# First attention head loaded by GpSimd, plain FFN units stored raw, two more w_o tiles kept, a new order at the tail

## The chip, the cores and the metric

The kernel runs on one core of a Trainium2 chip. The metric is the time of one execution on the device in microseconds (us), as the median of several. The engines run side by side, each through its own instructions in order, and wait for each other by semaphores: TensorE (matmuls), VectorE, ScalarE, GpSimd, and SyncE (SP), which here only issues DMAs. The profile is one execution seen by the hardware profiler. In it PE is TensorE, PEld its weight loads, DVE VectorE, ACT ScalarE, POOL GpSimd, SPq the queue of SP.

## The reference

One layer of a streaming encoder on 1024 prompt frames and 32 frames of running streams (1056 columns in all), model width 1024, in fp32:

```
p = x @ w_in                  # conv GLU pair | q | k | v | forget logits | 2 x gate
conv:  a*sigmoid(b) -> causal depthwise conv, 31 taps -> LayerNorm -> swish -> w_conv_out
attn:  softmax(q.k/8 + sum of log forget gates, causal) @ v -> w_attn_out   # 8 heads of 64
m   = sigmoid(g_conv)*y_conv + sigmoid(g_attn)*y_attn
x1  = LN1(alpha*x + m @ w_o)
x2  = LN2(alpha*x1 + relu(x1 @ w_up)^2 @ w_down)       # 4096 hidden channels
```

The rows k, v, log f and the last conv inputs are outputs too.

## The kernel before

Activations lie transposed: a tile holds 128 channels on partitions and frames along the row. Each fp32 operand is split into a high and a low half ("hi" by a ScalarE copy into fp32r, "lo" by a VectorE subtraction), and each product is three matmuls (hi hi, hi lo, lo hi), written by `mm3` and `dense`. A generator-driven planner (`Issue`, with a clock of its own for each engine) fixes the order of the instructions on TensorE, VectorE, ScalarE and GpSimd as the program text runs: background work is slipped in when its planned due time has come (`service`, `due`), filler work for TensorE when an operand isn't due yet (`fill`). A `margin` adds to a due time. The DMAs on SP get their order from the framework's scheduler, and run strictly in it.

**Stages.** (1) To 245 us: the input projections; VectorE runs the 31-tap convolution over `u` and `ca` in the background, on into stage 2. (2) To 325: gate tiles 0 to 5. Each gate product is copied from PSUM to `gt` by ScalarE and stored to DRAM (`g_s`). (3) 325 to 590: attention, head by head, with the rest of the gate products as filler; here `gt` has two buffers, and two PSUM banks ("acc") take the filler's products. Head h needs `k1, q1, k2, q2, v`, loaded by `load_head`; rows 64 to 127 of k2 and q2 hold constants (k2 ones; q2 zeros with two rows of ones) and the cumulated forget gates. The SBUF pool "b" of this stage begins where the pools "conv" and "a" lay; a tile waits for what was there. While GpSimd is the split engine (`W.engine = "pool"`) it computes the low halves of weights. (4) To 667: merge. (5) To 762: `w_o`, column blocks of 264 frames in the groups (0, 2), (1,), (3,). Weights pass through a ring of 4 raw and 4 split tiles (`Weights`: `load`, `split`, `take`, `limit` for how far it may read ahead); the odd w_o tiles are kept for all groups, the even ones (0, 2, 4, 6) loaded and split again for each. LN1 of each block runs in the background (`norm_steps`; `emit` makes `x_bh`, `x_bl`). (6) To 838: the plain FFN units: hidden tiles f = 0 to 5 for 4 blocks, 24 products `up`, each Relu, Square, hi, lo, stored to `hp_s` (`rest`, `second_half`, tile "spp"). The first 16 Relu results are held in tiles "d0", "d1". `combine` prepares sums for the next stage. (7) 838 to 1350: the rest of the FFN by a seven-product scheme (`S.step` makes the split weights, `go`/`product` the products in 4 PSUM bank pairs, VectorE adds them up; `residual` adds alpha*x1 as `extra`, one step per product). (8) To the end: `combined` sums, the plain units' down-projection `ps_dn` for three column blocks of 352 (`down_first`, `more`), with the w_down tiles `wd` (two for each pair of output tiles), and LN2 with the last block written out separately.

A gate product is stored by `g = staging.tile([P, CH], F32, tag=tag, bufs=bufs, ...)`, `act(g, ps, AF.Copy)`, `dma(g_s[m, :, chunks[c]], g)`. LN2's due times have `margin = 0.0 if tag >= MUS else NMARGIN` with NMARGIN = 2000 (ns).

Of the kernel before, what the change touches and what calls it, by code (L numbers as in the profile page):

```python
# [17 lines left out]
P = 128  # L18
# [54 lines left out]
NPL = 3  # L73
PAIRS = (*range(4, 15), 3, 15)
# [11 lines left out]
class Issue:  # L86
# [186 lines left out]
def hybrid_layer(ctx: ExitStack, tc, io):  # L273
# [24 lines left out]
    hp_s = [tc.dram_tile([P, 2, T], F32, name=f"hp{i}_s") for i in range(4 * (NFB - NKB))]  # L298
# [21 lines left out]
    plan += [io["w_o"][m] for _ in range(2) for m in range(0, KD, 2)]  # L320
# [487 lines left out]
    with pool("b") as pb, pool("pb", space=PSUM) as psb:  # L808
        k2s, q2s = [], []
        for i in range(2):  # L810
# [7 lines left out]
        sq = [pb.tile([P, 2 * (P + DEC)], F32R, name=f"sq{i}") for i in range(2)]  # L818
        sqv = [t.rearrange("p (n x) -> p n x", n=2)[:, :, 0:DEC] for t in sq]
        sq1, sq2 = ([t[:, 0:P], t[:, P:2 * P]] for t in sq)  # L820
        for t in sq:
            nc.gpsimd.memset(f32(t), 0.0)
        dma(sqv[1][DH:DH + 2], k2s[0][DH:DH + 2, 0:2 * DEC].rearrange("p (n x) -> p n x", n=2))
# [7 lines left out]
        def load_s():  # L831
            for i, t in enumerate(("sh", "sl")):
                for k in range(4):
                    yr[t].append(row(4 * i + k, f"y{t}{k}"))
            for cs in chunks:
                for k in range(4):
                    for i, t in enumerate(("sh", "sl")):
                        dma(yr[t][k][:, cs], s_s[i][k, :, cs])

        def early():  # L840
            for k in range(min(3, len(folded) // 2)):
                load_o(k)
            for m in range(YM):
                yw.append(W.take())
                yc.append(row(14 + m, f"yc{m}", F32))
                for c in range(NCH):
                    terms = y_terms(0, m, c)
                    yield [t for t4 in terms for t in t4]
                    ps = bbank(f"yc{m}_{c}")[:, :CH]
                    for last in mm3(ps, terms):  # L850
                        if not last:
                            yield None
                    act(yc[m][:, chunks[c]], ps, AF.Copy)
                    yield None

        I.filler.append([gates(range(GA, 16), bbank, pb, "g", GB, load_s), None])
        I.filler.append([early(), None])

        def load_head(h, i):
            hr = slice(h * DH, (h + 1) * DH)
            k1 = pb.tile([P, 2 * NKS], F32R, tag="k1", bufs=2, name=f"k1_{h}")
            q1 = pb.tile([P, SEQ], F32R, tag="q1", bufs=2, name=f"q1_{h}")
            k2, q2 = k2s[i % 2], q2s[h % 2]
            v = pb.tile([P, 10, P], F32R, tag="v", bufs=2, name=f"v_{h}")
            dma(k1[0:DH, 0:SEQ], qk_s["kh"][hr, 0:SEQ])
            dma(k1[DH:P, 0:SEQ], qk_s["kh"][hr, 0:SEQ])
            dma(q1[0:DH], qk_s["qh"][hr, 0:SEQ])
            dma(q1[DH:P], qk_s["ql"][hr, 0:SEQ])  # L870
            dma(k2[0:DH, 0:SEQ], qk_s["kl"][hr, 0:SEQ])
            dma(k2[DH:DH + 2, 0:SEQ].rearrange("s (t i) -> s t i", i=P), crows[0][h, :, 0:NT, :])
            dma(q2[0:DH], qk_s["qh"][hr, 0:SEQ])
            dma(q2[DH + 2:DH + 4, :].rearrange("s (t i) -> s t i", i=P), crows[1][h, :, 0:NT, :])
# [4 lines left out]
        def load_cached(g, i):  # L879
            k1 = pb.tile([P, 2 * NKS], F32R, tag="k1", bufs=2, name=f"sk1_{g}")  # L880
            k2 = k2s[i % 2]
            v = pb.tile([P, 10, P], F32R, tag="v", bufs=2, name=f"sv_{g}")
# [38 lines left out]

        units = []
# [4 lines left out]
        loaded = {}  # L927
# [164 lines left out]
        def work():  # L1092
            load(0)
# [135 lines left out]
    with pool("ps1", space=PSUM) as bank_pool[0]:  # L1229
# [54 lines left out]
        with pool("l1") as ln_pool[0]:  # L1284
            LNW, LNQ = CB, 2
            xrs = []
# [56 lines left out]
            for group in GROUPS:  # L1343
                sums = {}
                for m in range(KD):
# [11 lines left out]
                    if m % 2:  # L1357
# [17 lines left out]
            ws, pending, held_r = [], [], []  # L1375

            def rest():

                if pending:
                    r, f, b = pending.pop(0)  # L1380
                    act(r, r, AF.Square)
                    sp = ln_pool[0].tile([P, 2, CB], F32R, tag="spp", bufs=3, name=f"spp{f}_{b}")
# [14 lines left out]
            for n, (f, b) in enumerate(order):  # L1397
# [22 lines left out]
                for _ in range(0 if n < 8 else 1 if 12 <= n < 16 or n > 18 else 2):  # L1420
# [39 lines left out]
    loaded, hs = {}, []  # L1460
# [426 lines left out]
```

## Time and profile before

| | us |
|---|---|
| median of 3 runs | 1474.54 (1473.98 to 1475.47) |
| the profiled execution | 1471.28 |
| its span, first to last instruction | 1469.5 |
| TensorE busy | 1434.3 |
| VectorE busy | 1135.2 |
| ScalarE busy | 678.5 |
| GpSimd busy | 153.1 |

Busy times are of one engine over the span and overlap each other. The mean granted TensorE clock was 0.992 of full speed. A wait is listed as the engine and tile that waited, what released it, the total, the count and the longest. A row of a timeline is start, length, engine, line, operation, tiles and shapes, and in brackets the idle time before it.

### The profile page before, as it was taken

How to read it: one execution, taken by the hardware profiler on the slowest of the kernel's cores; microseconds unless marked ns; L12 is line 12 of the kernel's file. 1: busy time of each engine (PE TensorE's matmuls, PEld its weight loads, DVE VectorE, ACT ScalarE, POOL GpSimd, SP SyncE). 2: the span in 40 equal slices, each digit the busy share in tenths (PEclk: the TensorE clock that was granted, in tenths of full speed). 3: DMA queues.
4: the chain of work that ended last, by engine and by line, in shares of the span. 5: the costliest groups of instructions: out<-in, count | busy, mean ns of one | idle time of the engine just before them, and what ended most of it. 6: DMA issues, size and time to landing. Idle time of an engine off the chain costs nothing.

```text
span 1469.5 us, 28027 instructions
## 1 busy us (share of the span) xinstructions
PE 1434.3 (98%) x10632; PEld 1408.5 (96%) x10632; DVE 1135.2 (77%) x1925; ACT 678.5 (46%) x1425; POOL 153.1 (10%) x203
## 2 busy tenths in 40 slices
PE   9999999998999999999999999999999999999996
PEld 8999999997989999999999999999999999999995
DVE  6999899864666655856697988888976788879668
ACT  5113433455655656533356766676657322213223
POOL 0000000003355543000000000000000000000125
PEclk9999999999999999999999999999999999999998
DMA  7125544267555557435353448766689887775112
GB/s 244 45 67 155 171 167 151 89 219 197 157 146 139 153 148 263 140 99 177 109 166 119 144 153 296 253 240 234 226 295 343 328 323 253 274 270 175 44 40 79
DMA packets 156277, 267.87 MB, mean 182 GB/s; under 512 B 22506, under 2 KB 79082, under 8 KB 156142
## 3 DMA queue, kind: packets, MB, share of 16 engines
q1 hardware_dynamic: 156142, 266.08, 54.7%
q8 instruction: 84, 1.38, 0.4%
q14 instruction: 51, 0.42, 0.1%
HBM read 169.30 MB, written 96.66 MB: 181 GB/s over the span
## 4 chain that ended last, share of the span: by engine, by line
PE 86%; DVE 7%; ACT 2%; DMA 2%; issue 2%; SPq 0%; POOL 0%; DVEq 0%; ACTq 0%; POOLq 0%
PE ps_u L211 18%; PE ps_d L211 15%; PE ps_g L211 10%; PE ps_o L211 6%; PE ps_dn L211 4%; PE ps_v L211 4%; PE ps_yc L211 3%; PE ps_k L211 3%; PE ps_glua L211 3%; PE ps_q L211 3%; PE ps_glub L211 3%; PE ps_s L211 3%; PE ps_yo L211 2%; PE ps_pv L211 2%; PE ps_up L211 2%; PE ps_tr L215 2%
## 5 line engine op out<-in xcount | busy, mean ns | idle before, releaser
L240 DVE SCALAR_TENSOR_TENSOR ca<-u,prm,ca 128x1086 f32<-128x1086 f32 x120 | 161.7, 1347 | 2.4
L223 ACT ACTIVATE swhi<-s 128x512 fp32r<-128x512 f32 x100 | 61.7, 624 | 170.4 <-DVE s L232 154.0
L211 PE MATMUL ps_g<-xh,whi 128*128 128x352 f32 x384 | 132.4, 345 | 7.2 <-ACT gt L223 7.2
L211 PE MATMUL ps_g<-xh,wlo 128*128 128x352 f32 x384 | 124.2, 324 | 0.0
L211 PE MATMUL ps_g<-xl,whi 128*128 128x352 f32 x384 | 122.0, 324 | 0.0
L211 PE MATMUL ps_u<-tl,swhi 128*128 128x264 f32 x416 | 118.4, 285 | 0.0
L211 PE MATMUL ps_u<-th,swlo 128*128 128x264 f32 x416 | 118.3, 284 | 0.0
L211 PE MATMUL ps_u<-th,swhi 128*128 128x264 f32 x416 | 118.2, 284 | 0.0
L223 ACT ACTIVATE whi<-raw 128x512 fp32r<-128x512 f32 (+1 forms) x132 | 76.3, 623 | 65.5 <-PE ps_glua L211 31.6
L232 DVE TENSOR_TENSOR tl<-ps_tr,th 128x512 fp32r<-128x512 f32 (+2 forms) x96 | 51.0, 552 | 58.4 <-ACT th L223 57.7
L223 ACT ACTIVATE r<-r 128x528 f32<-128x528 f32 (+1 forms) x128 | 77.1, 602 | 37.8 <-DVE r L232 35.5
L211 PE MATMUL ps_d<-hu_h,swhi 128*128 128x264 f32 x480 | 92.9, 285 | 0.4 <-DVE aux L232 0.4
L211 PE MATMUL ps_d<-hu_l,swhi 128*128 128x264 f32 x480 | 92.8, 285 | 0.0
L232 DVE TENSOR_TENSOR wlo<-raw,whi 128x512 fp32r<-128x512 f32 (+1 forms) x112 | 72.6, 686 | 22.1 <-ACT whi L223 20.9
L232 DVE TENSOR_TENSOR r<-r,ps_u 128x528 f32<-128x528 f32 x91 | 62.6, 700 | 29.7 <-PE ps_u L211 29.4
L232 POOL TENSOR_TENSOR lnsum_n<-acc,acc 128x352 f32<-128x352 f32 x2 | 1.9, 943 | 790.8 <-DVE acc L232 790.8
L211 PEld LDWEIGHTS ps_g<-xh,whi 128*128 128x128 f32 x384 | 73.2, 191 | 8.3 <-ACT gt L223 7.5
L211 PEld LDWEIGHTS ps_u<-th,swhi 128*128 128x128 f32 x416 | 78.3, 188 | 0.0
L211 PEld LDWEIGHTS ps_u<-th,swlo 128*128 128x128 f32 x416 | 78.3, 188 | 0.0
L211 PEld LDWEIGHTS ps_u<-tl,swhi 128*128 128x128 f32 x416 | 78.2, 188 | 0.0
L211 PEld LDWEIGHTS ps_d<-hu_h,swhi 128*128 128x128 f32 x480 | 74.6, 189 | 0.6 <-issue 0.6
L211 PEld LDWEIGHTS ps_d<-hu_l,swhi 128*128 128x128 f32 x480 | 74.6, 189 | 0.0
(420 smaller groups left out, 5032.3 us busy)
## 6 DMA issues: line engine op xcount, KB each, us to landing
h_s<-sp SPq DMA_DIRECT2D x84, 528.0 KB
raw<-in_w_in_dram SPq DMA_DIRECT2D x64, 256.0 KB
hu_h<-h_s SPq DMA_DIRECT2D x30, 528.0 KB
hu_l<-h_s SPq DMA_DIRECT2D x30, 528.0 KB
sraw<-in_w_up_dram SPq DMA_DIRECT2D x52, 256.0 KB
hu<-h_s SPq DMA_DIRECT2D x24, 528.0 KB
sraw<-in_w_ds_dram SPq DMA_DIRECT2D x48, 256.0 KB
g_s<-gt SPq DMA_DIRECT2D x48, 176.0 KB
```

The lines of the kernel that those rows point to most:

```text
L211: self.nc.tensor.matmul(ps, lhsT=w, rhs=x, start=start, stop=stop)
L215: self.nc.tensor.transpose(ps, x, ident)
L223: self.nc.scalar.activation(out, in_, func, **kw)
L232: (self.nc.vector if eng == "dve" else self.nc.gpsimd).tensor_tensor(out, a, b, op)
L240: self.nc.vector.scalar_tensor_tensor(out, a, s, b, op0, op1)
```

## The change

- Head 0's loads move from SP's queue to GpSimd's, except v's, and are written ahead of the other attention work; the pool's first tiles are now k2_0, q2_0, k1_0, q1_0, v_0, then k2_1, q2_1 and the `sq` tiles. The ones of k2 and q2 are written by GpSimd memsets; three small DMAs that copied ones go.
- In the plain FFN, units f = 0 to 3 are stored raw after their Relu (`hp_s` one half as large); they are loaded again late (`late_hs`, from block 4, second half, step 3 on), squared and split there. Units 4 and 5 keep the old way.
- w_o tiles 2 and 4 are kept too, in "d0" and "d1"; only 0 and 6 are loaded again.
- LN2's due times get the margin of 2000 ns.
- One PSUM bank pair is passed over at the start of the down products; w_down is read ahead by another schedule, and four tiles instead of two are taken before the last `combined` sums.

```diff
+NLATE = 4
+WO_AGAIN = (0, 6)
-    def dma(self, out, in_):
+    def dma(self, out, in_, queue=None):
...
-        self.nc.sync.dma_start(out, in_)
+        (queue or self.nc.sync).dma_start(out, in_)
...
-    plan += [io["w_o"][m] for _ in range(2) for m in range(0, KD, 2)]
+    plan += [io["w_o"][m] for _ in range(2) for m in WO_AGAIN]
...
+        def constants(i):
             k2 = pb.tile([P, 2 * NKS], F32R, name=f"k2_{i}")
-            nc.vector.memset(f32(k2[DH:P, :]), 1.0)
+            nc.gpsimd.memset(f32(k2[DH:P, :]), 1.0)
             q2 = pb.tile([P, SEQ], F32R, name=f"q2_{i}")
             nc.gpsimd.memset(f32(q2[DH:P, :]), 0.0)
-            dma(q2[DH:DH + 2, :], k2[DH:DH + 2, 0:SEQ])
+            nc.gpsimd.memset(f32(q2[DH:DH + 2, :]), 1.0)
...
+            queue = nc.gpsimd if h == 0 else None
-            dma(k1[0:DH, 0:SEQ], qk_s["kh"][hr, 0:SEQ])
+            dma(k1[0:DH, 0:SEQ], qk_s["kh"][hr, 0:SEQ], queue)
...
             dma(v[:, 0:NT, :], v_s[h])
...
+        constants(0)
+        first_head = load_head(0, 0)
+        constants(1)
...
+        for t in sq:
+            nc.gpsimd.memset(f32(t), 0.0)
+        nc.gpsimd.memset(f32(sqv[1][DH:DH + 2]), 1.0)
...
-        margin = 0.0 if tag >= MUS else NMARGIN
+        margin = NMARGIN
...
+            for n, m in enumerate(m for m in range(0, KD, 2) if m not in WO_AGAIN):
+                kept[NWO + m] = lambda n=n, m=m: [ln_pool[0].tile([P, T], F32R, tag=f"d{n}", bufs=2, name=f"{x}_wo{m}") for x in ("whi", "wlo")]
...
-                if n < 16:
-                    if n % 4 == 0:
-                        held_r.append(ln_pool[0].tile([P, T], F32, tag=f"d{n // 8}", bufs=2, name=f"r{n}"))
-                    r = held_r[-1][:, n % 4 * CB:(n % 4 + 1) * CB]
+                r = tmp("rp", 5, f"r{f}_{b}")
+                act(r, ps, AF.Relu)
+                if f < NLATE:
+                    dma(hp_s[f][:, cblocks[b]], r)
                 else:
-                    r = tmp("rp", 3, f"r{f}_{b}")
-                act(r, ps, AF.Relu)
-                pending.append((r, f, b))
+                    pending.append((r, f, b))
...
+    def late_hs():
+        last = []
+        for f in range(NLATE):
+            hs[f] = unit(f"hs{f}", 6 + f)
+            parts = [[t[:, n * 2 * CB:(n + 1) * 2 * CB] for t in hs[f]] for n in range(2)]
+            raw = [pd.tile([P, 2 * CB], F32, tag="x1r", bufs=2, name=f"hr{f}_{n}") for n in range(2)]
+            if last:
+                tt(*last.pop(), SUB)
+            for n in range(2):
+                dma(raw[n], hp_s[f][:, n * 2 * CB:(n + 1) * 2 * CB])
+            yield
+            for n in range(2):
+                act(raw[n], raw[n], AF.Square)
+                act(parts[n][0], raw[n], AF.Copy)
+            tt(parts[0][1], raw[0], f32(parts[0][0]), SUB)
+            last.append((parts[1][1], raw[1], f32(parts[1][0])))
+            yield
+        tt(*last.pop(), SUB)
...
+        pair_bank("skip")
         for kb in range(NKB):
...
-                    if kb == NKB - 1 and g == 0 and 0 < i < 6:
-                        load_hs(i - 1, 5 + i)
+                    if (kb, g, i) == (NKB - 2, 1, 3):
+                        extra = chain(extra, late_hs())
...
-                        W.limit = NPLAN + (1, 1, 2, 3, 3, 4, 5)[i]
+                        W.limit = NPLAN + (1, 1.5, 1.5, 2, 3, 4, 4)[i]
                         W.ahead()
-        for _ in range(2):
+        for _ in range(4):
             wd.append(W.take())
```

## Rows read from the trace of the kernel before

**Rows 1.** The page: busy us, share of the span, instructions; DMA queues.

```profile
PE 1434.3 (98%) x10632; PEld 1408.5 (96%) x10632; DVE 1135.2 (77%) x1925; ACT 678.5 (46%) x1425; POOL 153.1 (10%) x203
...
q1 hardware_dynamic: 156142, 266.08, 54.7%
```

**Rows 2.** Busy time by stage: us, busy us (instructions), clock, DMA share, GB/s.

```profile
667.00:762.00 95.00, 95.00 (x778) 94.67 (x778) 72.51 (x159) 37.21 (x72) 0.00 (x0) 1.00 0.52 161
...
838.00:1330.00 492.00, 492.00 (x4039) 492.00 (x4040) 404.12 (x640) 243.98 (x426) 0.00 (x0) 1.00 0.75 264
```

**Rows 3.** Waits: TensorE's over the span, ScalarE's 333 to 341; us, times, longest.

```profile
PE ps_g L211 <- ACT gt L223: 7.2, 1, 7.2
...
PE ps_dn L211 <- DVE wk_l L232: 2.2, 1, 2.2
...
PE ps_var_n L211 <- DVE lnvar_n L232: 2.0, 2, 1.0
...
PE ps_dn L211 <- DVE acc L232: 1.3, 2, 0.9
...
ACT gt L223 <- DMA g_s<-gt: 14.0, 1, 14.0
```

**Rows 4.** Busy time by stage, around the first head.

```profile
286.40:300.00 13.60, 13.60 (x87) 13.60 (x86) 10.96 (x14) 7.04 (x13) 0.00 (x0) 1.00 0.34 116
...
300.00:325.60 25.60, 25.60 (x162) 25.45 (x161) 17.69 (x34) 15.30 (x32) 0.37 (x1) 1.00 0.72 235
...
340.60:344.60 4.00, 3.95 (x15) 3.85 (x16) 0.92 (x4) 2.05 (x6) 2.52 (x2) 0.50 0.44 123
```

**Rows 5.** The chain of waits, 285 to 341: start us, us, what.

```profile
285.75 0.61 PE ps_var_c L211 x2
...
317.21 1.86 DMA g_s<-gt
...
326.24 6.65 DMA k<-kh_s
...
334.97 5.06 DMA g_s<-gt
...
340.65 2.13 PE ps_g L211 x6
```

**Rows 6.** GpSimd's timeline, to 330: start us, us, operation, its idle time before.

```profile
264.55 0.95 POOL L814 MEMSET q<- 64x1024 f32 x1 [124.05 <-DVE ca L240]
...
315.95 0.37 POOL L822 MEMSET sq<- 128x320 f32 x1 [50.02 <-DVE csl L232]
```

**Rows 7.** Busy time by stage, around 800 us.

```profile
798.70:802.00 3.30, 1.61 (x7) 0.91 (x6) 2.53 (x8) 2.53 (x7) 0.00 (x0) 1.00 0.73 249
...
802.00:805.40 3.40, 3.39 (x14) 3.22 (x15) 3.22 (x7) 1.29 (x3) 0.00 (x0) 0.50 0.56 196
```

**Rows 8.** The chain of waits, around 798 us.

```profile
797.85 2.67 DMA hp_s<-spp
```

**Rows 9.** Timelines of VectorE and of TensorE, 778 to 798 us.

```profile
778.29 0.90 DVE L240 SCALAR_TENSOR_TENSOR acc<-acc,prm,rstd_n 128x264 f32<-128x264 f32 x2
...
784.89 0.49 DVE L240 SCALAR_TENSOR_TENSOR x_1l<-acc,prm,x_1h 128x264 fp32r<-128x264 f32 x1 [0.18 <-ACT x_1h L223]
...
793.07 0.49 DVE L240 SCALAR_TENSOR_TENSOR acc<-acc,prm,rstd_n 128x264 f32<-128x264 f32 x1
...
797.78 0.28 PE L211 MATMUL ps_up<-x_3h,whi 128*128 128x264 f32 x1
```

**Rows 10.** Busy time, the stretch in which the changed kernel squares late.

```profile
1300.70:1327.00 26.30, 26.30 (x218) 26.30 (x217) 21.18 (x34) 5.37 (x9) 0.00 (x0) 1.00 0.60 217
```

**Rows 11.** VectorE's timeline, 1354 to 1366 us.

```profile
1354.57 0.70 DVE L232 TENSOR_TENSOR acc<-acc,aux 128x528 f32<-128x528 f32 x1
...
1365.22 1.28 DVE L232 TENSOR_TENSOR wk_l<-raw,wk_h 128x512 fp32r<-128x512 f32 x2
```

**Rows 12.** Busy time, the last block's end.

```profile
1442.00:1456.00 14.00, 13.18 (x72) 11.20 (x70) 12.21 (x23) 5.37 (x11) 5.48 (x6) 1.00 0.08 27
```

More of the change, by code (lines that the diff above doesn't have):

```diff
@@ L297, in hybrid_layer @@
     h_s = [[tc.dram_tile([P, 2, 2, 2, CB], F32, name=f"h{b}_{i}_s") for i in range(7)] for b in range(NKB)]
-    hp_s = [tc.dram_tile([P, 2, T], F32, name=f"hp{i}_s") for i in range(4 * (NFB - NKB))]
+    hp_s = [tc.dram_tile([P, T] if i < NLATE else [P, 2, T], F32, name=f"hp{i}_s") for i in range(4 * (NFB - NKB))]
     o_s = [tc.dram_tile([H * DH, T], F32, name=f"o{i}_s") for i in range(2)]
@@ L828, in bbank @@
             return psb.tile([P, 512], F32, tag="acc", bufs=2, name="ps_" + name)
[L831 to L854, printed above, removed]
@@ L874, in load_head @@
-            dma(q2[DH + 2:DH + 4, :].rearrange("s (t i) -> s t i", i=P), crows[1][h, :, 0:NT, :])
+            v = pb.tile([P, 10, P], F32R, tag=f"v{i % 2}", bufs=1, name=f"v_{h}")
+            queue = nc.gpsimd if h == 0 else None
+            dma(k1[0:DH, 0:SEQ], qk_s["kh"][hr, 0:SEQ], queue)
+            dma(k1[DH:P, 0:SEQ], qk_s["kh"][hr, 0:SEQ], queue)
+            dma(q1[0:DH], qk_s["qh"][hr, 0:SEQ], queue)
+            dma(q1[DH:P], qk_s["ql"][hr, 0:SEQ], queue)
+            dma(k2[0:DH, 0:SEQ], qk_s["kl"][hr, 0:SEQ], queue)
@@ L920, in load_cached, with load_s, early @@
             return k1, k2, sq1, sq2, v
+        constants(0)
+        first_head = load_head(0, 0)
+        constants(1)
+        sq = [pb.tile([P, 2 * (P + DEC)], F32R, name=f"sq{i}") for i in range(2)]
+        sqv = [t.rearrange("p (n x) -> p n x", n=2)[:, :, 0:DEC] for t in sq]
+        sq1, sq2 = ([t[:, 0:P], t[:, P:2 * P]] for t in sq)
+        for t in sq:
+            nc.gpsimd.memset(f32(t), 0.0)
+        nc.gpsimd.memset(f32(sqv[1][DH:DH + 2]), 1.0)
+        def load_s():
+            for i, t in enumerate(("sh", "sl")):
+                for k in range(4):
+                    yr[t].append(row(4 * i + k, f"y{t}{k}"))
+            for cs in chunks:
+                for k in range(4):
+                    for i, t in enumerate(("sh", "sl")):
+                        dma(yr[t][k][:, cs], s_s[i][k, :, cs])
+        def early():
+            for k in range(min(3, len(folded) // 2)):
+                load_o(k)
+            for m in range(YM):
+                yw.append(W.take())
+                yc.append(row(14 + m, f"yc{m}", F32))
+                for c in range(NCH):
+                    terms = y_terms(0, m, c)
+                    yield [t for t4 in terms for t in t4]
+                    ps = bbank(f"yc{m}_{c}")[:, :CH]
+                    for last in mm3(ps, terms):
+                        if not last:
+                            yield None
+                    act(yc[m][:, chunks[c]], ps, AF.Copy)
+                    yield None
+        I.filler.append([gates(range(GA, 16), bbank, pb, "g", GB, load_s), None])
+        I.filler.append([early(), None])
         units = []
@@ L926, in hybrid_layer @@
                 units.append(("cached", h - 2))
-        loaded = {}
+        loaded = {0: first_head}
         def load(n):
@@ L1092, in work @@
         def work():
-            load(0)
             for n, (kind, h) in enumerate(units):
@@ L1356, in hybrid_layer @@
                         W.drop()
-                    if m % 2:
+                    if m not in WO_AGAIN:
                         wk[m] = w
@@ L1381, in rest @@
                     act(r, r, AF.Square)
-                    sp = ln_pool[0].tile([P, 2, CB], F32R, tag="spp", bufs=3, name=f"spp{f}_{b}")
+                    sp = ln_pool[0].tile([P, 2, CB], F32R, tag="spp", bufs=2, name=f"spp{f}_{b}")
                     act(sp[:, 0, :], r, AF.Copy)
@@ L1419, in hybrid_layer @@
                         next(sums, None)
-                for _ in range(0 if n < 8 else 1 if 12 <= n < 16 or n > 18 else 2):
+                if len(pending) > 1:
                     rest()
@@ L1458, in x_op @@
         return get
-    loaded, hs = {}, []
+    loaded, hs = {}, {}
     places = [("quad", 2 + n, 0) for n in range(2)] + [("quad", n, half) for half in range(2) for n in range(2)]
@@ L1663, in hybrid_layer @@
                         load_h()
-                    if kb == NKB - 1 and g == 0 and 0 < i < 6:
-                        load_hs(i - 1, 5 + i)
+                    if (kb, g, i) == (NKB - 2, 1, 3):
+                        extra = chain(extra, late_hs())
+                    if (kb, g, i) == (NKB - 1, 0, 6):
+                        for _ in extra:
+                            pass
+                        for f in range(NLATE, 5):
+                            load_hs(f, 6 + f)
                     if end:
```

31 lines of the change are left out of this document (9 added, 22 removed).

## The prediction

> **What bounds the kernel now.** I read the page's table of busy time first: TensorE is busy in 1434.3 of 1469.5 us [rows 1], so at most 35 us can be had, and only where TensorE stands or runs slowly. The table by stage shows where it doesn't: from 667 to 762 us and from 838 to 1330 us it is busy in every microsecond [rows 2]. Work that the change takes from VectorE or ScalarE there gives nothing. The list of what TensorE waited for [rows 3] names the rest: one wait of 7.2 us for a gate tile, 2.2 us for the split of a w_down tile, twice 1.0 us for a variance, and 1.3 us in two waits for PSUM banks of the last matmuls. Two more stretches are in the windows: at half the granted clock (1.2 GHz) it ran from 340.6 to 344.6 us, behind the 7.2 us wait [rows 4], and from 802.0 to 805.4 us, behind a stretch of 3.3 us in which it was busy for 1.61 [rows 7].
>
> **Part A, the first head's loads.** TensorE's 7.2 us wait is for the ScalarE copy of a gate bank, and that copy waited 14.0 us for the store of an older gate tile to land (there are two such tiles) [rows 3]. The store was issued at 334.97 and took 5.06 us; a sister issued at 317.21 took 1.86 [rows 5]. It came so late because SP works in order: the head's loads stand ahead of it from 326.24 [rows 5]. The change takes eleven DMAs out of SP's way there: two copies of ones into q2, one into sq, and eight loads of head 0; only v's load stays. The store is then issued some 8.5 us earlier, at about 326.5. Even if it still takes 5.06 us it has landed at 331.6, before TensorE runs out of banks at 333.4 (it went on at 340.65 [rows 5], less 7.2). So the wait goes whole, 7.2 us, and with it the slow clock: 3.95 us of work at half rate is 2.0 us lost [rows 4]. Sum: 9.2 us.
>
> Are the loads themselves in time? On GpSimd they stand behind the memsets of k2 and q2. The new layout puts k2_0, q2_0, k1_0 and q1_0 over the old mean tile and the conv inputs. The conv inputs are free by 264.6, when the second q2 memset ran in the kernel before [rows 6]; the mean tile is last read by the variance matmul that ends at 286.4 [rows 5]. Three memsets of about 0.95 us each [rows 6] bring GpSimd to 289.3. No DMA of the kernel before was issued by GpSimd (queue q1 is SP's alone [rows 1]), so its price has to be bounded: from below by nothing, from above by 5.06 us each, the slowest landing here, if one waited for the other: 8 x 5.06 + 289.3 = 329.8. The first scores come about 334 (in the kernel before they followed six gate matmuls behind the wait [rows 5]). I take 1.5 us each, near the longest GpSimd memset of that kind; done by about 303. Cover is some 30 us, and the whole price is hidden; the DMA engines are at 0.34 and 0.72 of their time from 286 to 325 [rows 4]. GpSimd then waits for the last conv tiles (about 324; the sq memset at 315.95 waited for such a one [rows 6]), does four more memsets and is free by 329. Behind these stands only its next weight split, 2.5 us, which in the kernel before ran at 341 [rows 4]. What is late next is the softmax chain of head 0, as it was before.
>
> The Trainium skill, SBUF — State Buffer, section "SBUF: two separate sides", speaks against this part: descriptors of a DMA that GpSimd issues can't be written while VectorE runs an operation in a two-port mode, such as a plain fp32 copy. VectorE is busy in 10.96 of 13.6 us and in 17.69 of 25.6 us of the stretch [rows 4], but with two-input operations and reciprocals, for which the same page (its summary by port) names no two-port mode for tensor_tensor. No GpSimd DMA in the trace of before shows it. By that rule at its worst the loads go out only after VectorE's last operation; what this would cost is the slower rival below.
>
> **Part B, the plain FFN units.** From 798.7 to 802.0 TensorE lost 1.7 us, and the slow clock after it another 1.7 (half of 3.39) [rows 7]. It waited for the last normalised block, whose ScalarE steps stood behind "spp" tiles waiting for a store to land, 2.67 us [rows 8]. In the changed kernel 16 of the 24 units make no such tile: ScalarE does their Relu alone, 32 activations and 16 VectorE subtractions are gone, and SP stores the raw tile. Without them VectorE goes through the block as it did through the one before it, 16 operations in 7.1 us (from 778.29 to 785.38) from 793.07 on [rows 9]: done by 800.2. TensorE came to the block at 797.78 [rows 9] and takes three matmuls of 492 / 4039 = 0.122 us [rows 2] per tile, so it needs the eighth at 800.3. Sum: 3.4 us; between 1.7 (a rest of the wait keeps the clock low) and 4. Two more w_o tiles kept spare eight halves of a load and a split, all where TensorE is full [rows 2]: nothing.
>
> The work comes back in the last block of the FFN: eight halves are loaded raw, squared, copied (ScalarE is busy in 5.37 of 26.3 us there) and subtracted: 8 x 0.70 (the row of 128 x 528 [rows 11]) = 5.6 us of VectorE between 1300.7 and 1327, where it is busy in 21.18 of 26.3 us [rows 10]. It fits only just: 5.1 us were free. A product of 12 matmuls takes 1.46 us and there are four bank pairs, so TensorE feels a lag only after three products, 4.4 us; nothing is lost there, but I let VectorE enter the next stretch 1 us late (0 to 3).
>
> **Part C, the start of the last matmuls.** From 1330 to 1366 VectorE is the bound. Its order puts the last two "combined" groups (1354.57 to 1365.2) ahead of the split of w_down tile 3 (the first is tile 0) at 1365.22 [rows 11], and TensorE waits 2.2 us for it [rows 3]. With four tiles taken first, the split comes 10 us earlier, and the skipped bank pair makes the first banks wait for an older addition (the longer of those two waits, 0.9 us [rows 3]). TensorE went on about 1365.9 and had 24 matmuls of 0.16 us (25.6 us / 162 of the same width [rows 4]) to tile 4, 1369.8; it now gets there 3.1 us earlier, at 1366.7. Then tile 4's split is late: it follows the combined groups, which two more halves push to 1366.5, so its first half (0.64) ends at 1367.1, a wait of 0.4. Less 1 us brought from part B: 1.7, or 2 us where one of the smaller waits goes as well (from -1 to 3.5).
>
> **Part D, the margin in the last norms.** Both matmuls of a norm are now placed 2 us later than planned. The two waits of 1.0 us go [rows 3]. The first chain has room. The second one ends up to 4 us later, and VectorE has work for 12.21 of the 14 us to 1456 [rows 12], so the outputs of block 1 that haven't been written by then compete with the last block: from 0 to 4 us of it come back at the end. I take 1.5. Sum: a gain of 0.5 (from -2 to 2).
>
> **The sum.** 9.2 + 3.4 + 2.0 + 0.5 = 15.1 us. The profiled execution took 1471.28 us around its span of 1469.5; less 15.1 it would take 1456.2. The median of the runs shown is 3.26 us above that execution, so the median to expect is 1459.4 us.
>
> **Rivals.**
> 1. VectorE full. The late squares put TensorE on hold in the last FFN block, and the second norm's delay comes back whole. For it: 5.1 us free against 5.6 needed. Against it: four bank pairs and weights split four products ahead. Parts C and D are then -1 and -2: 9.2 + 3.4 - 3 = 9.6 us gained, 1464.9.
> 2. Another wait takes the head's place. The gate stores are no longer held, but something else is not there at 333 (head 0's v, still on SP, or a gate weight): half of part A returns with the slow clock. 4.6 + 5.9 = 10.5 gained, 1464; if the whole returns, 5.9, 1468.6. Against it: nothing else waited at that point [rows 3], and the tiles that v covers are free by about 316 [rows 6].
> 3. Slower: GpSimd's issue starves. Its loads start only when VectorE's conv work ends, about 324.4, and cost d each in a row: TensorE waits 324.4 + 8d + 5.06 - 334.2 = 8d - 4.7 us, and 2 us of slow clock. This is worse than the 9.2 us it replaces and the 5.9 gained elsewhere from d = 2.2 us on. At 3 us it gives 19.3 + 2 - 15.1 = 6.2 us slower, 1480.7. At 1.6 it still leaves 5 us gained, 1469.4. For it: no row prices d. Against it: 2.2 us would be over twice a GpSimd memset of 64 x 1024 [rows 6].
> 4. The change doesn't reach what it names: the slow clock stays in both places (3.7 us) though the waits go. 1463.
>
> Another rule, DMA: Bandwidth & Descriptors, section "Issuing engines are not separate DMA queues", says that issuing from another engine saves only the sequencer's time, since all transfers share the same 16 DMA engines. By it the 5.06 us landing need not shorten. The sum above holds with that landing too.
>
> **How the numbers follow.** The forecast as worked out, 1455 to 1463: 0.63. Rival 1: 0.13; rival 2: 0.10; rival 4: 0.04; rival 3: 0.05, of which 0.04 slower than before. The last 0.05 is for better than 1455, where nothing of parts C and D comes back (9.2 + 4 + 3.5 + 2 = 18.7 gained, 1455.8) and one of the waits I have not named goes too. The range from 1453.5 to 1467 leaves out less than 2 in 10. About 0.2% (3 us) is what a measurement of this kernel can tell from no change. Faster by more than that: 0.93; within: 0.03; slower: 0.04.
>
> **What would show it.** In the changed kernel's trace: no TensorE wait for a gate copy near 333 and full clock from 325 to 360 (A); eight GpSimd DMAs issued from about 289, landed well before 334; no wait for x_3 and full clock around 800 (B); VectorE close to full from 1285 to 1315 with no TensorE wait for it; no wait for w_down tile 3, a short one for tile 4 (C); no waits at the variances, and outputs of block 1 among the last block's additions (D). I am wrong if TensorE still stands at the first scores, if GpSimd takes over 2 us per load, or if TensorE waits on VectorE in the last FFN block.

## The result, and the profile after

The changed kernel takes 1464.17 us (median of 4, 1461.97 to 1467.44), the kernel before beside it 1474.87: ratio 0.993, 95% interval 0.991 to 0.9949. So 10.7 us were gained (7.5 to 13.3) where 15.1 were forecast; the time lies in the range of the prediction, but outside its forecast case (1455 to 1463), and next to the prices of two rivals: 1464.9 of rival 1 (VectorE full) and 1464 of rival 2 (half of part A lost), of which the waits below leave only the first. A later set of runs of the same kernel gave 1463.21 (E11).

First the page's table of busy time and the queue that is new, and then the longest of TensorE's waits (total, times, longest), of the changed kernel; the one of 1.9 us for `tl` and two of 1.0 us and less for `yg` that are left out stand in the kernel before too:

```profile
PE 1433.0 (98%) x10632; PEld 1409.1 (96%) x10632; DVE 1126.6 (77%) x1906; ACT 672.5 (46%) x1403; POOL 160.7 (11%) x215
...
q0 software_dynamic: 544, 1.59, 0.4%
```

```profile
PE ps_md_last L213 <- DVE lnsum L234: 4.1, 1, 4.1
PE ps_dn L213 <- DVE acc L234: 2.0, 1, 2.0
...
PE ps_d L213 <- DVE aux L234: 1.7, 1, 1.7
...
PE ps_d L213 <- ACT hs L225: 1.4, 1, 1.4
```

The 7.2 us for a gate tile, the 2.2 us for the split of w_down tile 3 and both waits for a variance [rows 3] are gone, and so is the wait for x_3 near 800 us, which the kernel before had:

```profile
PE ps_up L211 <- ACT x_3h L223: 1.3, 1, 1.3
```

Four others stand in their place, 4.1 + 2.0 + 1.7 + 1.4 = 9.2 us, all in the last 150 us. Where each stands, from TensorE's timeline (start, us, what, and in brackets the idle time before it):

```profile
1315.47 0.48 PE L213 MATMUL ps_d<-hu_h,swhi 128*128 128x264 f32 x2 [1.44 <-ACT hs L225]
...
1335.24 0.48 PE L213 MATMUL ps_d<-hu_h,swhi 128*128 128x264 f32 x2 [1.71 <-DVE aux L234]
...
1345.69 0.43 PE L213 MATMUL ps_dn<-hs_h,whi 128*128 128x352 f32 x1 [2.02 <-DVE acc L234]
...
1445.58 1.12 PE L213 MATMUL ps_md_last<-lnsum,mean_d 128*128 128x352 f32 x2 [4.13 <-DVE lnsum L234]
```

The next table is worked out from the records of TensorE's matmuls in all thirteen traces: the time from the end of the last matmul of one kind to that of the next. "head" runs from the conv norm's last variance to the last score, "up" is norm 1 with the up products of the plain units, "down" the ps_d products, "last" the ps_dn products, "end" from there to the last variance. The stretches that it leaves out agree within 0.7 us, but for the first 17 us of an execution, which differ by up to 2.7 us between these thirteen.

```
us                          head    up     down   last    end
                        var_c-s   o-up    u-d   d-dn   dn-var_last
before                   283.97  75.52  246.69  102.94  2.62
before, second trace E8  287.92  77.01  248.23  104.50  2.63
changed                  275.36  71.11  250.37   99.84  7.71
changed, second     E11  274.86  71.10  250.15   98.29  7.72
E1                       274.73  71.10  249.92  101.54  2.62
E2                       276.31  71.10  247.48   99.84  7.83
E3                       274.69  71.10  248.44   99.96  7.96
E4                       286.38  71.10  252.02   99.91  7.85
E5                       274.75  71.10  249.63  100.23  2.63
E6                       274.73  71.10  249.58  100.21  7.71
E7                       274.75  71.10  248.15   99.10  2.63
E9                       275.02  74.92  248.09   97.23  7.97
E10                      274.68  71.10  248.04   97.58  3.65
```

The first two columns are part A and part B near 800 us, and they gained 8.6 and 4.4 us between the two first traces, where 9.2 and 3.4 were forecast. Of the last three columns together the kernel before needed 352.25 us in its first trace, the changed one 357.92 and 356.16: what parts B (its late half), C and D did from 1100 us on cost 4 to 6 us, where a gain of 2.5 was forecast. From the last score to the last w_o product both kernels take 191.4 us: the two more w_o tiles that are kept gain nothing there, as forecast.

### The profile page after: what moved, and what is told of

It reads as the page before. It is cut to its first block, busy times and chain, and to the rows that moved or that the text cites. A ratio compares the mean times of both kernels' runs of the same rounds, so it can differ in the third digit from the quotient of the medians.

```text
span 1462.5 us, 27944 instructions
## 1 busy us (share of the span) xinstructions
PE 1433.0 (98%) x10632; PEld 1409.1 (96%) x10632; DVE 1126.6 (77%) x1906; ACT 672.5 (46%) x1403; POOL 160.7 (11%) x215
## 4 chain that ended last, share of the span: by engine, by line
PE 89%; DVE 6%; DMA 2%; ACT 2%; issue 1%; SPq 0%; POOL 0%; DVEq 0%; ACTq 0%
PE ps_u L213 18%; PE ps_d L213 14%; PE ps_g L213 10%; PE ps_o L213 6%; PE ps_dn L213 5%; PE ps_up L213 5%; PE ps_v L213 4%; PE ps_glub L213 3%; PE ps_yc L213 3%; PE ps_k L213 3%; PE ps_glua L213 3%; PE ps_q L213 3%; PE ps_s L213 3%; PE ps_yo L213 2%; PE ps_pv L213 2%; PE ps_tr L217 2%
## 5 line engine op out<-in xcount | busy, mean ns | idle before, releaser
L225 ACT ACTIVATE whi<-raw 128x512 fp32r<-128x512 f32 (+1 forms) x120 | 69.4, 623 | 69.3 <-PE ps_glua L213 31.6
L225 ACT ACTIVATE r<-r 128x528 f32<-128x528 f32 (+1 forms) x112 | 70.6, 630 | 38.4 <-DVE r L234 36.2
L234 DVE TENSOR_TENSOR wlo<-raw,whi 128x512 fp32r<-128x512 f32 (+1 forms) x100 | 64.8, 686 | 25.9 <-ACT whi L225 24.7
```

What stands on the lines that cost most here:

```text
L225: self.nc.scalar.activation(out, in_, func, **kw)
L234: (self.nc.vector if eng == "dve" else self.nc.gpsimd).tensor_tensor(out, a, b, op)
```

## The experiments

E1 to E11 below. Each time stands beside runs of the kernel before on the same chip (medians 1473.83 to 1474.58), as a ratio with its 95% interval; the stage lengths are in the table above.

**E1, no margin in the last norms.**

```
-        margin = NMARGIN
+        margin = 0.0 if tag >= MUS else NMARGIN
```

> The margin of 2 us is taken out of the last norms again (as before), all else as in the changed kernel (1464.2 us). Theory M (the margin moves block 1's outputs behind the last block's additions and so makes the new 4.1 us TensorE wait for lnsum): that wait goes, the two waits of 1.0 us for the variances return: 4.1 - 2.0 = 2 us faster, 1462. Theory L (the 4.1 us are VectorE's lag out of the late squares, carried to the end): the wait stays and the two of 1.0 us return: 2 us slower, 1466.

Measured: 1460.87 us, 0.9918 (0.9904 to 0.9931). The 4.1 us are gone and the two waits of 1.0 us are back, as theory M has it; theory L falls. The longest of TensorE's waits of this kernel:

```profile
PE ps_dn L213 <- DVE acc L234: 2.5, 2, 2.0
PE ps_var_n L213 <- DVE lnvar_n L234: 2.0, 2, 1.0
```

From the last ps_d matmul to the last variance this kernel takes 104.16 us, the changed one 106.01 in E11, whose clock stayed up at the start of the last matmuls as it did here: the margin costs 1.85 us.

How it does that is seen in VectorE's order around the last block's first step. "lnpart" is subtracted there from the last block's tiles, and "rstd_n" is the factor of block 1's outputs. The kernel before, and then the changed one:

```profile
1431.31 2.35 DVE L244 RECIPROCAL rstd_n<-rstd_n 128x352 f32<-128x352 f32 x1 [1.54 <-ACT rstd_n L223]
1433.77 1.31 DVE L240 SCALAR_TENSOR_TENSOR acc<-acc,prm,rstd_n 128x352 f32<-128x352 f32 x1
...
1440.42 0.97 DVE L236 TENSOR_SCALAR acc<-acc,prm 128x352 f32<-128x352 f32 x1
1441.32 2.45 DVE L232 TENSOR_TENSOR acc<-acc,lnpart 128x352 f32<-128x352 f32 x2
```

```profile
1423.98 2.35 DVE L246 RECIPROCAL rstd_n<-rstd_n 128x352 f32<-128x352 f32 x1 [2.25 <-ACT rstd_n L225]
1428.45 1.71 DVE L234 TENSOR_TENSOR acc<-acc,lnpart 128x352 f32<-128x352 f32 x2 [2.12 <-ACT lnpart L225]
...
1437.60 1.27 DVE L242 SCALAR_TENSOR_TENSOR acc<-acc,prm,rstd_n 128x352 f32<-128x352 f32 x1
...
1442.77 1.25 DVE L242 SCALAR_TENSOR_TENSOR acc<-acc,prm,rstd_n 128x352 f32<-128x352 f32 x1
...
1444.38 0.52 DVE L234 TENSOR_TENSOR acc<-ps_dn,acc 128x352 f32<-128x352 f32 x1
1444.99 0.53 DVE L234 TENSOR_TENSOR lnsum<-lnsum,acc 128x352 f32<-128x352 f32 x1
```

Before, four pairs of block 1's output operations (1433.77 to 1441.3) stood ahead of the subtraction of lnpart. In the changed kernel VectorE stands idle from 1426.33 to 1428.45 for lnpart, and all of its output operations of block 1 (from 1436.29 to 1444.46, with three such pairs) come after it, among the last block's own additions. The last but one of those additions, 1444.38, and the sum behind it, 1444.99, are what TensorE waits for until 1445.58.

**E2, late units loaded, not squared.**

```
...
-                dma(raw[n], hp_s[f][:, n * 2 * CB:(n + 1) * 2 * CB])
+                dma(parts[n][0], hp_s[f][:, n * 2 * CB:(n + 1) * 2 * CB])
+                dma(parts[n][1], hp_s[f][:, n * 2 * CB:(n + 1) * 2 * CB])
...
-                act(raw[n], raw[n], AF.Square)
-                act(parts[n][0], raw[n], AF.Copy)
-            tt(parts[0][1], raw[0], f32(parts[0][0]), SUB)
...
```

> The four late units are loaded raw into both halves and neither squared nor split (their squares are left out of the result); all else as in the changed kernel (1464.2 us). Theory M: VectorE, free of 8 subtractions (5.6 us) and of the 4.2 us in which it stood for ScalarE's squares, enters the last matmuls at least 4.4 us earlier; TensorE's waits at 1314 (1.4), 1333 (1.7) and 1343 (2.0) shrink to what VectorE's own work from 1330 to 1357 leaves: 4 to 5 us faster, 1459 to 1460, and the 4.1 us wait for lnsum stays. Theory L: the wait for lnsum goes as well: 8 us faster or more, 1456. If the late squares had fitted into VectorE's free time, as the prediction had it: 1 us, 1463.

Measured: 1462.09 us, 0.9922 (0.991 to 0.9935). The stage of the ps_d products is 247.48 us, 2.7 to 2.9 shorter than in the changed kernel; the waits of 1.4 and 1.7 us shrink to one of 0.5. So the late squares, with their subtractions, cost TensorE 2.8 us and not 4 to 5. Two other waits don't move: 2.07 us at 1343 and 4.13 us for lnsum. Neither comes of VectorE's lag out of the late squares.

**E3, the late subtractions one step further on.**

```
-            if last:
-                tt(*last.pop(), SUB)
+            while last:
+                tt(*last.pop(0), SUB)
...
-            tt(parts[0][1], raw[0], f32(parts[0][0]), SUB)
-            last.append((parts[1][1], raw[1], f32(parts[1][0])))
+            for n in range(2):
+                last.append((parts[n][1], raw[n], f32(parts[n][0])))
...
-        tt(*last.pop(), SUB)
+        while last:
+            tt(*last.pop(0), SUB)
```

> The subtractions of the late units are put one step further on in VectorE's order (both, behind ScalarE's four activations of that unit by a whole step); the amount of work is that of the changed kernel (1464.2 us). Theory S (VectorE's loss is the 4.2 us in which it stands at the head of its order for ScalarE): the stalls go, 3 to 4 us faster, 1460.5 to 1461. Theory W (it is the 5.6 us of added work, which don't fit): the stalls turn into waits elsewhere, within 1 us, 1463.5 to 1464.5.

Measured: 1461.75 us, 0.992 (0.9906 to 0.9933); the ps_d stage is 248.44 us, 1.8 shorter. So of the 2.8 us at least 1.8 are stalls of VectorE, and up to 1 is the added work: between the two theories, nearer to S. (Of the 4.2 us for which VectorE stood for ScalarE's copies, 1.6 are left in this kernel.) The stalls in the changed kernel, from the chain of waits and from VectorE's timeline:

```profile
1300.57 4.36 DMA hr<-hp_s
1305.01 0.65 ACT hr L225
1305.69 0.66 ACT hs L225
```

```profile
1299.84 0.71 DVE L234 TENSOR_TENSOR hs_l<-hr,hs_h 128x528 fp32r<-128x528 f32 x1 [1.37 <-ACT hs_h L225]
...
1306.36 0.71 DVE L234 TENSOR_TENSOR hs<-hr,hs 128x528 fp32r<-128x528 f32 x1 [1.49 <-ACT hs L225]
...
1314.05 0.71 DVE L234 TENSOR_TENSOR hs<-hr,hs 128x528 fp32r<-128x528 f32 x1 [1.37 <-ACT hs L225]
```

A raw half is loaded (4.36 us), squared and copied by ScalarE (0.65 each), and VectorE, which works in order, stands at the head of its own order for that copy: 1.37 + 1.49 + 1.37 = 4.2 us idle, with the additions that TensorE waits for behind it.

**E4, the first head's loads on SP.**

```
-            queue = nc.gpsimd if h == 0 else None
+            queue = None
```

> The first head's eight loads stay at their new, early place and over the same tiles, but are issued by SP. Theory Q (the queue matters: SP works in order, and these loads must wait for the mean tile, free at about 287): SP stands there from about 265 to 290, the stores of the gate tiles behind it come late, and TensorE waits some 10 us near 285: 1474, and at least 5 us slower than the changed kernel. Theory P (the place alone matters): within 1 us of 1464.2.

Measured: 1474.32 us, ratio 1.0 (0.9988 to 1.0011): all that the change gains is lost. Theory Q is right in its price and wrong in the place. SP did not stop at 265: it works through the stores of gate and conv tiles first, for whose makers it waits 36 and 5 us of the stretch from 262 to 345, comes to these loads only at 326, and the gate wait is back where it was. Two views of this kernel, TensorE's wait and the chain of waits ahead of it (start, us, what):

```profile
PE ps_g L213 <- ACT gt L225: 8.8, 1, 8.8
```

```profile
326.38 0.55 SPq L208
326.97 7.72 DMA k<-kh_s
334.77 6.96 DMA g_s<-gt
```

The load of k took 7.72 us. SP issued the eight loads and v's from 326.38 to 333.95, and the store of the gate tile, which stands behind them, only at 334.77 (334.97 in the kernel before). Written earlier in the program, these loads go out no earlier on SP (326.38, before 326.24), and their new tiles gain nothing; what gains is the queue of an engine that has nothing else to do. What an earlier place in SP's order would be worth, no run shows.

**E5, the margin for the first block alone.**

```
-        margin = NMARGIN
+        margin = 0.0 if tag > "n2_0" else NMARGIN
```

> The margin of 2 us is kept for the first of the last norms' two planned blocks and taken out for the second alone; all else as in the changed kernel (1464.2 us; 1460.9 with the margin out of both). Theory M2 (only the second block's outputs collide with the last block's additions): the wait for lnsum (4.1) goes, one variance wait (the second, 1.0) returns, the first (1.0) does not: 1 us faster than with no margin at all, 1459.9. Theory M1 (any delay in the chain is passed on to the end): no better than without margin, 1461 to 1463.

Measured: 1460.04 us, 0.99 (0.9885 to 0.9915). One variance wait is left (0.93 at 1415.5). From the last ps_d matmul to the end: 102.86 us, 1.3 less than in E1. Theory M2.

**E6, the old start of the last matmuls.**

```
-        pair_bank("skip")
...
-                        W.limit = NPLAN + (1, 1.5, 1.5, 2, 3, 4, 4)[i]
+                        W.limit = NPLAN + (1, 1, 2, 3, 3, 4, 5)[i]
...
-        for _ in range(4):
+        for _ in range(2):
```

> Two w_down tiles are taken ahead of the last combined groups, the limits are the old ones and no bank pair is skipped (as before); all else as in the changed kernel (1464.2 us). Theory G (this part gains, as the old waits of 2.2 us for the split of tile 3 and 1.0 us for banks return in place of the new one of 2.0 us): 1.2 us slower, 1465.4. Theory N (VectorE is the bound here, and what it does first is paid by what it does later): no change within 0.5 us. Theory H (taking four tiles first is what puts the last addition of block products 2 us late): 1 us faster, 1463.

Measured: 1463.61 us, 0.993 (0.9916 to 0.9944): theory N, no change. The bank wait of 2.0 us is there with the old start too, so theory H falls. The wait of 2.2 us for tile 3 does not come back. In the kernel before TensorE came to that tile 10.2 us after its wait for a bank (1353.5 to 1363.7); here that wait is 2.02 us and ends at 1343.4, and with 1.6 us for a stretch of slow clock behind it TensorE is there at 1355.2, when the first half of the split is done (1353.92 + 0.64).

**E7, three edits together.** E3, E5, and the last step of the combined groups behind the last additions:

```
-                    next(extra, None)
+                    if not end or i < 6:
+                        next(extra, None)
```

> Three edits on the changed kernel together: the late units' subtractions one step further on (2.2 us faster by itself from 100 us on), the margin for the first norm block alone, and the last step of the combined groups left until after the last products' additions, which stood behind it (two VectorE operations of 0.62 us each ahead of the addition for which TensorE waits 2.0 us). If the three add up: 2.2 + 4.4 + 1.2 = 7.8 us faster than the changed kernel, 1456.4. If VectorE is full from 1330 to 1357 whatever its order: the last edit gives nothing, 1457.6. If the tail gives back what is gained ahead of it: 1460.

Measured: 1456.14 us, 0.9874 (0.986 to 0.9888): they add up. The wait of 2.0 us at 1343 is 0.78. What stands ahead in the changed kernel, from VectorE's timeline: the two halves of a split (w_down tile 2) and two operations of a combined group (0.70 each by the row, 0.62 from start to start) come before the last product's additions, which free the bank. This edit takes the two operations away from there.

```profile
1341.88 1.29 DVE L234 TENSOR_TENSOR wlo<-raw,whi 128x512 fp32r<-128x512 f32 x2
1343.09 0.70 DVE L234 TENSOR_TENSOR acc<-acc,aux 128x528 f32<-128x528 f32 x1
1343.70 0.70 DVE L242 SCALAR_TENSOR_TENSOR acc<-x1r,acc 128x528 f32<-128x528 f32 x1
1344.32 1.31 DVE L234 TENSOR_TENSOR acc<-ps_d,acc 128x528 f32<-128x528 f32 x2
```

**E8, the kernel before once more** (no edit).

> The kernel before, unchanged, for a second trace of it. If executions differ only in their first 10 us (when TensorE gets its first x and w tiles: it ends the glua tiles at 100.6 in the first trace of before, between 100.4 and 103.1 in five others), the second trace has the same waits and stage lengths within 0.3 us from there on. If the kernel before has a wait that comes and goes, one stage of it differs by 2 us or more.

Measured: 1474.21 us, 0.9996 (0.9987 to 1.0005), but its profiled execution has a span of 1477.6 us, 8.1 above the first one. From 100 us on it is longer by 7.9: 4.0 in the head's stage (the gate wait is 8.4 us long, and the clock is slow near 413 us too), 1.5 in the up products, 1.5 in the ps_d products (a wait of 1.3 us at 1126 which the first trace doesn't have) and 1.6 in the last matmuls, less 0.7 in the ps_u products. In the last matmuls the clock fell behind the same wait of 2.2 us that left it alone in the first trace. Busy time by stage at the head and behind that wait, of the second trace and then of the first one (the granted clock is third from the end):

```profile
333.00:350.00 17.00, 8.57 (x39) 7.51 (x38) 3.00 (x11) 3.83 (x11) 2.52 (x2) 0.70 0.77 207
...
1373.00:1375.00 2.00, 2.00 (x8) 2.00 (x8) 1.31 (x3) 0.00 (x0) 0.00 (x0) 0.50 0.69 220
```

```profile
333.00:350.00 17.00, 9.78 (x55) 8.87 (x54) 5.00 (x15) 5.49 (x16) 2.52 (x2) 0.80 0.83 222
...
1366.40:1368.40 2.00, 2.00 (x14) 2.00 (x14) 1.30 (x3) 0.00 (x0) 0.00 (x0) 1.00 0.63 181
```

**E9, no raw units.**

```
-NLATE = 4
+NLATE = 0
...
-                    if (kb, g, i) == (NKB - 2, 1, 3):
-                        extra = chain(extra, late_hs())
-                    if (kb, g, i) == (NKB - 1, 0, 6):
-                        for _ in extra:
-                            pass
-                        for f in range(NLATE, 5):
-                            load_hs(f, 6 + f)
+                    if kb == NKB - 1 and g == 0 and 0 < i < 6:
+                        load_hs(i - 1, 5 + i)
```

> No FFN unit is stored raw (all six plain ones are squared and split when they are made, as before) and the last block loads them split; the first head's loads, the kept w_o tiles, the start and the margin of the last matmuls stay as in the changed kernel (1464.2 us). Theory B (the gain near 800 us is that ScalarE makes 32 activations and 16 stores fewer there): the wait for x_3 is back, the stage of the up products is 75.5 to 77.0 us long as in the two traces of before (71.1 with raw units), and the last FFN block, without late squares, is 2.9 us shorter: 1.5 to 3 us slower, 1466. Theory K (it comes of the w_o tiles kept, or of the earlier store order): the up stage stays at 71 us and only the 2.9 us are gained: 1461.

Measured: 1463.35 us, 0.992 (0.9904 to 0.9936). The up stage is 74.92 us, 3.8 longer, with short waits and the slow clock near 793; the ps_d stage is 2.2 shorter and the last matmuls wait 0.87 us in place of 2.0. Theory B is right on the up stage, and yet no difference in the total can be measured: what raw units save near 800 us, they cost again after 1100. Theory K falls. Busy time by stage of this kernel (columns as in [rows 2], the granted clock third from the end):

```profile
790.00:796.00 6.00, 5.20 (x29) 4.06 (x28) 5.02 (x11) 3.97 (x10) 0.00 (x0) 0.90 0.56 191
796.00:806.00 10.00, 10.00 (x76) 10.00 (x76) 6.82 (x13) 6.70 (x15) 0.00 (x0) 0.89 0.35 114
```

The shorter wait at the start of the last matmuls goes with the place of tile 2's split in VectorE's order. In the kernel before (first pair of rows) and here (second pair) its two halves stand behind the last product's additions, and the bank wait is 0.9 us. In E6 (third pair), as in the changed kernel and in E2, they stand ahead of them, and it is 2.0:

```profile
1352.14 1.31 DVE L232 TENSOR_TENSOR acc<-ps_d,acc 128x528 f32<-128x528 f32 x2
1353.37 1.28 DVE L232 TENSOR_TENSOR wlo<-raw,whi 128x512 fp32r<-128x512 f32 x2
```

```profile
1344.43 1.32 DVE L234 TENSOR_TENSOR acc<-ps_d,acc 128x528 f32<-128x528 f32 x2
1345.66 1.28 DVE L234 TENSOR_TENSOR wlo<-raw,whi 128x512 fp32r<-128x512 f32 x2
```

```profile
1339.60 1.29 DVE L234 TENSOR_TENSOR wlo<-raw,whi 128x512 fp32r<-128x512 f32 x2
...
1342.05 1.32 DVE L234 TENSOR_TENSOR acc<-ps_d,acc 128x528 f32<-128x528 f32 x2
```

So this wait came with the raw units, not with their squares (E2) and not with the new start (E6). Why the split changes places with them, no run shows.

**E10, as E7 with half the margin for the second block** (`NMARGIN / 2` in place of 0.0).

> As the three edits together (1456.1 us), with half the margin (1 us) instead of none for the second norm block. If half the margin suffices: the last wait for a variance, 0.9 us, goes without more, 1455.2. If any delay moves outputs of that block behind the last block's additions (they stand in VectorE's order behind lnpart by two pairs more): the wait for lnsum is back, 2 to 4 us slower than without, 1458 to 1460.

Measured: 1455.01 us, 0.9865 (0.9851 to 0.9878), the lowest median here, 9 us below the changed kernel and level with E7 within the spread of the two. The wait of 0.9 us for a variance is gone; one of 0.8 us for lnsum is there. Two of TensorE's waits of this kernel:

```profile
PE ps_dn L213 <- DVE acc L234: 0.8, 1, 0.8
PE ps_md_last L213 <- DVE lnsum L234: 0.8, 1, 0.8
```

**E11, the changed kernel once more** (no edit).

> The changed kernel, unchanged, for a second trace. Theory C (whether the clock falls to half after the same 2.0 us wait near 1344 differs from execution to execution; it did in the first trace of this kernel and not in two others with the same wait): stage lengths equal within 0.3 us, except those where the clock falls in one of the two traces and not in the other, by 1.6 to 1.9 us each. The head's stage (287 to 563 us) stays at 274.7 to 276.3 us, against 284.0 and 287.9 of before.

Measured: 1463.21 us, 0.9923 (0.9907 to 0.9939). All stages agree with the first trace within 0.5 us (0.3 was expected), except the last matmuls, 1.55 shorter: theory C. Busy time by stage behind the wait of 2.02 us, in the first trace and then in the second:

```profile
1347.60:1349.60 2.00, 2.00 (x8) 2.00 (x8) 1.90 (x4) 1.65 (x3) 0.00 (x0) 0.50 0.67 219
```

```profile
1346.00:1352.00 6.00, 6.00 (x39) 6.00 (x39) 5.90 (x11) 3.02 (x5) 0.00 (x0) 1.00 0.39 128
```

## Why the prediction came out as it did

**A was right in its mechanism, with nothing to spare.** TensorE's wait for the gate copy is gone and the clock stays up (busy time by stage of the changed kernel):

```profile
333.00:350.00 17.00, 16.88 (x113) 15.11 (x112) 10.79 (x25) 10.98 (x28) 5.72 (x8) 1.00 0.85 241
```

GpSimd's part is shown by its timeline in the same trace:

```profile
289.52 0.95 POOL L819 MEMSET q<- 2x1024 f32 x1
290.42 1.23 POOL L208 DMA_DIRECT2D k<-kh_s  x2
...
294.26 0.64 POOL L208 DMA_DIRECT2D q<-c_s  x1
...
326.42 0.14 POOL L902 MEMSET sq<- 2x64 f32 x1
335.25 2.55 POOL L234 TENSOR_TENSOR wlo<-raw,whi 128x512 fp32r<-128x512 f32 x2 [8.68 <-ACT whi L225]
```

Eight loads go out from 290.42 to 294.90, 0.5 to 0.6 us each, where 1.5 were taken; they land within 3.7 to 6.2 us (medians by tile); GpSimd is free at 326.6 and its next split, at 335.25, waits for ScalarE alone. The bound from above was read wrongly: 5.06 us is not the slowest landing in the rows, the load of k took 6.65 [rows 5], and 8 x 6.65 + 289.3 = 342.5 is past the first scores. What the loads cost here made that of no account. Rival 3 (starved issue) falls: VectorE was busy in 3.47 of the 4.6 us in which they were issued (busy time by stage; VectorE's is the third of the busy columns),

```profile
290.40:295.00 4.60, 4.60 (x31) 4.60 (x30) 3.47 (x4) 2.67 (x4) 4.50 (x9) 1.00 0.68 170
```

and no issue took longer than 0.64 us. VectorE's four operations there were one reciprocal and three scalar_tensor_tensor. The Trainium skill, SBUF — State Buffer, section "SBUF: two separate sides", warns of operations in a two-port mode, such as a plain fp32 copy; none of these is a plain copy, and the blocking is shown by no run here.

The gate store, forecast to go out at 326.5 and to land at 331.6, went out at 327.88 and landed at 334.03, 6.15 us later (this trace runs 1.1 us behind that of before from its first matmuls on). ScalarE's copy waited 6.9 us for it, to 334.13, and TensorE lost 0.1 us: the forecast had some 1.8 us to spare, and none were left. The Trainium skill, DMA: Bandwidth & Descriptors, section "Issuing engines are not separate DMA queues", has all transfers share the same 16 DMA engines, so that another issuing engine saves only the sequencer's time, which it calls usually small beside the transfer. The trace agrees in that the landing did not get shorter. It differs on what is saved: in E4 the nine issues took SP 7.6 us (326.38 to 333.95), all of it ahead of the store, and the head's stage is 11.0 to 11.5 us longer.

The size of A could not be told from one trace of before: 8.6 us between the two first traces, where 9.2 were forecast, but 13.1 against the second trace of before (E8, E11).

**B was half right.** Near 800 us the gain was 4.4 us and not 3.4: the wait went (E9 brings short waits and the slow clock back). The 1.7 us lost from 798.7 to 802.0 was read from TensorE's busy time, 1.61 of 3.3 us; but the 7 matmuls there [rows 7] are only 0.85 us of work at 0.122 each, so some 2.4 were lost, and with the 1.7 for the slow clock 4.1. The step that failed is "nothing is lost there, but I let VectorE enter the next stretch 1 us late". It set 5.6 us of work against 5.1 free, and left out that VectorE would stand for ScalarE's copy and the load before it. Price on TensorE: 2.8 us (E2), at least 1.8 of it those stalls (E3). By the prediction's own sign ("if TensorE waits on VectorE in the last FFN block") it was wrong here. With the raw units also came the longer bank wait at the start of the last matmuls, 2.0 us for 0.9 (E9), which no part of the prediction has.

**C failed.** A gain of 2.0 was forecast, and in this kernel the part is worth 0 (E6). The wait for tile 3 went, but it goes with the old start too; and the bank wait, forecast to be one of the old ones of 1 us at most, is 2.0 us with either start. VectorE is the bound there (busy in 34.96 of the 36 us from 1330 to 1366), and ahead of the last product's additions stand tile 2's split (E9) and two operations of a group which nobody waits for yet: without these two the wait is 0.8 (E7). What part C would have been worth without the raw units, no run shows.

**D failed with its sign.** "... from 0 to 4 us of it come back at the end. I take 1.5", a gain of 0.5 (from -2 to 2): both waits for a variance went as said, and the last matmuls end 3.25 us sooner than in E1 (98.29 against 101.54), but 5.1 us come back between them and the last variance (7.72 against 2.62): a loss of 1.85, inside the range, but with the other sign. Of the 5.1 the wait for lnsum is 4.1; most of the rest is half clock behind it (granted 0.51 from 1446.0 to 1449.2 in the first trace). More came back than the 4 us given as the most. The operations delayed do not just fill VectorE's free time: they fall behind an instruction that waits for something else.

**The sum.** With the measured terms: 8.6 + 4.4 for A and B, less 2.8 for the late squares, 0 for C and less 1.85 for D is 8.4 us; the first pair of traces differs by 8.1 from 100 us on, with 1.6 lost to a stretch of slow clock in the changed kernel (E11) and 0.7 gained in stretches that the change doesn't name; some 0.6 us are not accounted for. That is one pair of traces: the second pair (E8, E11) differs by 18.0 from 100 us on, and the medians lie between. The medians differ by 10.7, since the profiled execution of before was a short one: all its timed runs took longer, by 2.7 to 4.2 us, and E8 shows where such time can sit: 5.4 of its 7.9 us are in the two stages from which the change takes the waits. So the 3.26 us that the forecast added belonged in part to before alone; the changed kernel's own profiled execution took 1464.28, about its median. Rival 1 named the place (late squares, second norm) and came to 1464.9, by a smaller gain of A and B and a smaller loss at the end than were measured. That the measured time lies so near its price, and inside the stated range, is in part luck: two errors of opposite sign.

## What to carry to other kernels

A load moved to an idle engine's queue is worth the time for which the old queue holds what stands behind it; written earlier on the old queue, it went out no earlier here (E4). Where TensorE stands, count its matmuls and not its busy time to see what was lost. When work is moved to a stage with free time on an in-order engine, price the stalls that its inputs bring, each with all that stands behind it, and not the added work alone. Where a delay is added ahead of one step, list which instructions change places behind it on every engine: here, at the end of the kernel, they changed places with the last ones.

## What the runs showed of the hardware

The clock did not answer alike to like waits. Behind a TensorE wait of 2.0 to 2.2 us at the start of the last matmuls it fell to 1.2 GHz (granted 0.50) for some 3 us in E2, E3, E4, E6, E8 and the first trace of the changed kernel, and stayed at 2.4 GHz (1.00) in E1, E5, E11 and the first trace of before. E7, E9 and E10, with waits of 0.8 to 0.9 us there, kept 1.00. A wait of 1.9 us near 400 us stands in all thirteen traces, and the clock fell behind it in E2 and E8 alone (E2's head stage is 1.6 us longer than that of E3). Behind the wait of 4.1 us for lnsum it was at 0.50 in all seven traces that have it. So a wait of some 2 us has two prices, 2.0 and 3.6 us, and which one is paid differs between executions of one program.

The Trainium skill, TensorE: Matmul & The Clock Gate, section "What's actually happening", has the gate's observation running freely, not started by the kernel. The traces fit that in so far as the same wait was followed by either clock; they show no more of the cause.
